# Layer 1's output product with tokens on partitions, and the last norm along the free dimension

## The chip, the cores and the metric

The kernel runs on one core of a Trainium2 chip (trn2). The metric is the device time of one execution in microseconds; runs of the same kernel here lie within 0.1% of each other.

## The reference

Two transformer-like layers over 256 tokens of width 2048, with 256 context tokens beside them. Layer 0 mixes by short convolution and latent attention, layer 1 by grouped attention. What the change touches is the end of layer 1:

```python
y = (attn * silu(p[..., o_v:])) @ w_out                      # 256 x 2048 by 2048 x 2048
z = ALPHA * x + gate * y                                     # gate: one number per channel
mu = jnp.mean(z, axis=-1, keepdims=True)
var = jnp.mean(jnp.square(z - mu), axis=-1, keepdims=True)
x = (z - mu) * lax.rsqrt(var + EPS) * g + b                  # g, b: one number per channel
```

## The kernel before, in words

Channels lie on partitions and tokens along the free dimension from the first load to the store. A product of 2048 channels into 128 is made of 16 steps, one per 128 input channels. Every operand is split into a high and a low fp32r part, and each step is three matmuls (mm3, L128 to L130): high by high, high by low, low by high.

Weights come in transfers of 512 KB into one of three buffers (wraw, in wpieces), issued from SP's queue. A transfer is two pieces of 128 x 512; ACT casts a piece to its high part (L124), DVE subtracts it from the raw numbers for the low part (L125), and four pieces can be ready at a time (WPC). mtile runs the 16 steps of one output tile: here the weights stand still in TensorE and the 256 tokens move, 48 matmuls of 256 columns per tile.

Layer 1 ends with a loop over the 16 tiles of 128 output channels (lines 1130 to 1150). For each tile: the product into PSUM, DVE's residual z = gate * y + z (L1135), ACT's square (L1144), and POOL's running sums of z and of z squared (L1146, L1147). The sums over channels run across partitions, so TensorE makes them with a column of ones (colsum, L197): of tiles 0 to 14 during the last tile's steps, of the last tile behind its product. lnstats and rsqrt (three Newton steps, L180 to L188) work on 128 x 2 numbers on DVE; mean and rstd are broadcast over partitions by transposes (spread, L204), and then DVE, POOL and ACT centre, scale and finish 16 tiles of 128 x 256 (L1157, L1185, L1187, L1189) and SP issues nine stores.

The order of the work: each engine runs its own list of instructions from the front, one after the other, and waits where an operand or a buffer isn't ready. The lists are made at build time from the code's order; in this part of the program a scheduler may move an instruction ahead of others on its engine. PSUM has eight banks, handed out in turn. On DVE's list the splits of coming weights stand between the residuals.

## Time and profile before

| what | us |
|---|---|
| median of 3 runs | 1380.29 (1379.82 to 1380.78) |
| the profiled execution, its own time | 1381.53 |
| its span, first to last instruction | 1379.8 |
| PE busy, share of the span | 1335.0, 97% |
| DVE busy | 1103.2, 80% |
| ACT busy | 600.7, 44% |

The span leaves out what lies before the first and behind the last instruction, so it is shorter than the execution's own time. A busy PE is a PE with a matmul in its pipeline: matmuls overlap, so the time of one is read from start to start, not from its duration. The granted clock (PEclk) is a share of full speed: 1.00 is 2.4 GHz, 0.50 is 1.2 GHz.

### The profile page before, as it was taken

What the parts mean: (1) busy time and instruction counts of PE and PEld (TensorE: products, weight loads), DVE (VectorE), ACT (ScalarE), POOL (GpSimd) and SP (SyncE); (2) the same over time, 40 slices, a digit from 0 to 9 for tenths busy, and PEclk for the clock granted to TensorE, in tenths of its full rate; (3) what the DMA queues carried; (4) which work ended last, traced back from release to release, by engine and by line L of the source; (5) the groups of instructions that cost most, each with busy time, mean ns of one, the idle gap of its engine ahead of it and who ended that gap; (6) DMA issues with size and microseconds to landing.
All of it is one profiled execution on the core that took longest, in us unless ns stands there. A gap on an engine that the chain in (4) does not pass through costs nothing.

```text
span 1379.8 us, 21557 instructions
## 1 busy us (share of the span) xinstructions
PE 1335.0 (97%) x8068; PEld 1165.5 (84%) x8068; DVE 1103.2 (80%) x2037; ACT 600.7 (44%) x1163; POOL 136.1 (10%) x128
## 2 busy tenths in 40 slices
PE   7999999999999999999999999989999999999994
PEld 5667788888878888888888888878999999999994
DVE  7998578576689888888888888889688888887666
ACT  3233356444552222222224333444446666665553
POOL 3354310000000000000000000000330000000333
PEclk9999999999999999999999999999999999999997
DMA  9889412212177665576765688742123434344552
GB/s 366 318 297 340 180 62 77 85 39 84 62 259 247 231 224 215 218 253 214 246 226 177 225 309 329 261 152 81 47 92 124 137 128 144 127 140 137 184 184 77
DMA packets 74473, 251.74 MB, mean 182 GB/s; under 512 B 7616, under 2 KB 10560, under 8 KB 74112
## 3 DMA queue, kind: packets, MB, share of 16 engines
q1 hardware_dynamic: 73168, 243.48, 50.7%
q0 software_dynamic: 1200, 6.88, 1.3%
q8 instruction: 63, 1.03, 0.3%
q14 instruction: 42, 0.34, 0.1%
HBM read 248.24 MB, written 2.10 MB: 181 GB/s over the span
## 4 chain that ended last, share of the span: by engine, by line
PE 84%; DVE 10%; issue 2%; DMA 2%; ACT 1%; SPq 0%; POOL 0%; DVEq 0%; ACTq 0%; POOLq 0%
PE out L130 7%; PE out L128 6%; PE out L129 6%; DVE jk L331 4%; PE g L128 3%; PE g L129 3%; PE g L130 3%; PE q L129 2%; PE q L128 2%; PE q L130 2%; PE cg L130 2%; PE cg L129 2%; PE cg L128 2%; PE cc L129 2%; PE cc L128 2%
## 5 line engine op out<-in xcount | busy, mean ns | idle before, releaser
L124 ACT CAST wh<-wr 128x512 fp32r<-128x512 f32 x468 | 289.9, 621 | 484.1 <-PE out L129 134.2
L125 DVE TENSOR_TENSOR wl<-wr,wh 128x512 fp32r<-128x512 f32 x455 | 316.2, 702 | 140.4 <-ACT wh L124 138.2
L653 DVE CUSTOM_DVE_ANT_0 jk<-gr,sb 128x2048 bf16<-128x2048 f32 x112 | 255.8, 2284 | 4.3 <-DMA gr<-in_wmT_dram 4.1
L128 PE MATMUL out<-mh,wh 128*128 128x512 f32 (+1 forms) x288 | 105.5, 366 | 0.0
L130 PE MATMUL out<-mh,wl 128*128 128x512 f32 (+1 forms) x288 | 105.5, 366 | 0.0
L129 PE MATMUL out<-ml,wh 128*128 128x512 f32 (+1 forms) x288 | 105.2, 365 | 0.0
L129 PE MATMUL g<-xl,wh 128*128 128x256 f32 (+1 forms) x332 | 102.1, 308 | 0.0
L331 DVE CUSTOM_DVE_ANT_0 jk<-wt,srow 128x1024 bf16<-128x1024 f32 x64 | 96.0, 1499 | 5.8 <-DMA wt<-in_wmT_dram 4.1
L1047 POOL TENSOR_TENSOR z<-z,rl 128x256 f32<-128x256 f32 x16 | 13.1, 838 | 792.8 <-ACT rl L1045 792.8
L128 PE MATMUL g<-xl,wh 128*128 128x256 f32 x256 | 75.0, 293 | 0.0
L128 PE MATMUL out<-m1h,wh 128*128 128x256 f32 x256 | 72.5, 283 | 0.0
L129 PE MATMUL out<-m1l,wh 128*128 128x256 f32 x256 | 72.4, 283 | 0.0
L130 PE MATMUL out<-m1h,wl 128*128 128x256 f32 x256 | 72.4, 283 | 0.0
L130 PE MATMUL g<-xl,wl 128*128 128x256 f32 x256 | 72.3, 283 | 0.0
L129 PEld LDWEIGHTS g<-xl,wh 128*128 128x128 f32 x332 | 63.4, 191 | 2.8
L130 PE MATMUL q<-xl,wl 128*128 128x256 f32 x224 | 63.4, 283 | 0.0
L129 PE MATMUL q<-xl,wh 128*128 128x256 f32 x224 | 63.3, 283 | 0.0
L128 PE MATMUL q<-xl,wh 128*128 128x256 f32 x224 | 63.3, 283 | 0.0
L130 PEld LDWEIGHTS out<-mh,wl 128*128 128x128 f32 x288 | 54.3, 188 | 9.0 <-DVE wl L125 0.2
L129 PEld LDWEIGHTS out<-ml,wh 128*128 128x128 f32 x288 | 54.3, 188 | 8.8
L128 PEld LDWEIGHTS out<-mh,wh 128*128 128x128 f32 x288 | 54.3, 188 | 8.6
L130 PE MATMUL cg<-xh,wl 128*128 128x512 f32 x128 | 49.9, 390 | 0.8 <-DVE wl L125 0.8
(332 smaller groups left out, 3658.6 us busy)
## 6 DMA issues: line engine op xcount, KB each, us to landing
gr<-in_wmT_dram SPq DMA_DIRECT2D x64, 1024.0 KB, 5.0
wr<-in_w_o_dram SPq DMA_DIRECT2D x68, 512.0 KB, 3.4
wr<-in_w_g_dram SPq DMA_DIRECT2D x56, 512.0 KB, 3.3
wr<-in_w_c_dram SPq DMA_DIRECT2D x48, 512.0 KB, 4.2
wt<-in_wmT_dram SPq DMA_DIRECT2D x32, 512.0 KB, 6.6
wm<-in_wm_dram SPq DMA_DIRECT2D x32, 512.0 KB, 7.2
wr<-in_w_q_dram SPq DMA_DIRECT2D x32, 512.0 KB, 3.7
xr<-in_xT_dram SPq DMA_DIRECT2D x32, 256.0 KB, 5.8
```

Source lines behind the costliest of these rows:

```text
L124: S.copy(out=pr[0], in_=raw)
L125: (eng or V).tensor_tensor(out=pr[1], in0=raw, in1=f(pr[0]), op=ALU.subtract)
L128: TE.matmul(o, lhsT=a[0], rhs=b[0], start=start, stop=False)
L129: TE.matmul(o, lhsT=a[0], rhs=b[1], start=False, stop=False)
L130: TE.matmul(o, lhsT=a[1], rhs=b[0], start=False, stop=stop)
L331: V.tensor_tensor_reduce(out=junk, in0=rows[hf], in1=srow[v][:, hf * 1024:hf * 1024 + 1024], scale=1.0, scalar=0.0, op0=ALU.mult, op1=ALU.add,
L653: V.tensor_tensor_reduce(out=junk, in0=w, in1=sb[v], scale=1.0, scalar=0.0, op0=ALU.mult, op1=ALU.add, accum_out=dst[:, v:v + 1])
L1047: G.tensor_tensor(out=ax1[j], in0=ax1[j], in1=rl, op=ALU.mult)
```

## The change

The output product is turned round: 128 tokens stand still in TensorE (a column block of mix1) and the weights move. The 16 output tiles become five groups of 4, 4, 4, 2 and 2 tiles (OUT), so a step of a group of four is three matmuls of 512 columns for each of the two token halves. A weight piece is now one input block by four output tiles; each transfer still moves 512 KB, gathered from four places of w_o1 (opieces). The last group's weights are loaded and split during group 2 and kept in buffers of the normed input (xa, xlp) that is no longer read, and its product runs for the first 128 tokens, then for the second.

The output has tokens on partitions, so gate and residual input are turned into that layout by TensorE (turned, 12 transposes in each of the groups 0 to 3). The residual is DVE's multiply with the broadcast gate row and a fused add that also sums z; ACT squares z and sums too (residual). The norm's sums now run along the free dimension on 128 x 2 numbers. normalise(t) makes mean and rstd for one token half, normalises four pieces of 128 x 512, turns each back with four transposes, applies g and b (DVE and ACT, 128 x 128 each) and stores 256 KB per piece. POOL has no part in it. The buffers of keys and values are given back first (kvs.close()), and their room holds the new tiles.

```diff
@@ -36,7 +36,6 @@
 CJ, WSR, WMB, WTB, WQ, XF = 10, 2, 3, 4, 0, 2
 NA = 17
 SK, SR, WS1 = 6, 5, 3
-NPRE, NBET, POOLT, FIN = 3, 1, (3, 4, 6, 8, 11, 12), "AAVAAVAVAVAAAGAV"
 HA, HB, HC = 7, 10, 14
 QH, TH, GS = 4, 5, 3
 
@@ -940,7 +939,8 @@
                             mm3(acc[3 + tt], cols(xc[j], tt * P), cols(w, 0, T), j == 0, j == KT - 1)
             order_.close()
             cgs.close()
-            kvp = ctx.enter_context(right("kv", 18))
+            kvs = ctx.enter_context(ExitStack())
+            kvp = kvs.enter_context(right("kv", 18))
 
 
             dma(gcos, A["gcos"])
@@ -1119,79 +1119,115 @@
                 if h + 1 < NH1:
                     pes = scores1(h + 1, q)
 
-            s1 = s2 = None
-            ln1 = []
-
-            def early1(s1, s2):
-                ln1.append(psum("lst"))
-                colsum(ln1[0], s1, L, 0, "first")
-                colsum(ln1[0], s2, L, 2, "on")
-
-            for m in range(16):
+            kvs.close()
+            oz = ctx.enter_context(right("oz"))
+            grow = oz.tile([P, D], F32, name="grow")
+            zT = [oz.tile([P, D], F32, name=nm("zT")) for _ in range(2)]
+            part = [small.tile([P, 2, 5], F32, name=nm("pt"), tag="part%d" % t) for t in range(2)]
+            OUT = ((0, 4), (4, 4), (8, 4), (12, 2), (14, 2))
+            def opieces(m0, n, make):
+                per = 8 // n
+                for c in range(2):
+                    for i in range(n):
+                        r = wp.tile([P, 1024], F32, tag="wraw", name=nm("wr"), bufs=WRAW)
+                        dma(r.rearrange("p (m k) -> p m k", m=n),
+                            A["w_o1"][m0:m0 + n, c][:, :, i * per * P:(i + 1) * per * P].rearrange("m p k -> p m k"))
+                        rv = r.rearrange("p (m k n) -> p m k n", m=n, k=per)
+                        for u in range(per):
+                            pr = make()
+                            split(rv[:, :, u, :], tuple(x.rearrange("p (m n) -> p m n", m=n) for x in pr))
+                            yield pr
+            def ring_piece():
+                return (wp.tile([P, 512], F32R, tag="wh", name=nm("wh"), bufs=WPC),
+                        wp.tile([P, 512], F32R, tag="wl", name=nm("wl"), bufs=WPC))
+            kept = iter([xa] * 14 + [xlp] * 2)
+            def half_ring():
+                a, b_ = ring_piece()
+                return a[:, :L], b_[:, :L]
+            def kept_piece():
+                t = at(next(kept), F32R, "wo")
+                return t[:, :L], t[:, L:]
+            def turned(m0, n):
+                g_ps = psum("gr")
+                for i in range(n):
+                    TE.transpose(g_ps[:, i * P:i * P + P], gate1[:, m0 + i, :].broadcast_to([P, P]), ident)
+                S.copy(out=grow[:, m0 * P:(m0 + n) * P], in_=g_ps[:, :n * P])
+                for t in range(2):
+                    r_ps = psum("xt")
+                    for i in range(n):
+                        TE.transpose(r_ps[:, i * P:i * P + P], ax1[m0 + i][:, t * P:t * P + P], ident)
+                    S.copy(out=zT[t][:, m0 * P:(m0 + n) * P], in_=r_ps[:, :n * P])
+            def residual(t, i, ps):
+                m0, n = OUT[i]
+                sl = slice(m0 * P, (m0 + n) * P)
+                y = oz.tile([P, T], F32, tag="y", name=nm("y"), bufs=2)[:, :n * P]
+                V.tensor_tensor(out=y, in0=ps[:, :n * P], in1=grow[:, sl], op=ALU.mult)
+                V.tensor_tensor_reduce(out=zT[t][:, sl], in0=y, in1=zT[t][:, sl], scale=1.0, scalar=0.0,
+                                       op0=ALU.add, op1=ALU.add, accum_out=part[t][:, 0, i:i + 1])
+                S.activation(out=y, in_=zT[t][:, sl], func=AF.Square, accum_out=part[t][:, 1, i:i + 1])
+            def normalise(t):
+                e = small.tile([P, 2], F32, name=nm("e"), tag="le2")
+                V.reduce_sum(out=e, in_=part[t], axis=AX.X)
+                V.tensor_scalar(out=e, in0=e, scalar1=1.0 / D, scalar2=None, op0=ALU.mult)
+                q = small.tile([P, 1], F32, name=nm("q"), tag="lq1")
+                V.tensor_mul(q, e[:, 0:1], e[:, 0:1])
+                V.scalar_tensor_tensor(out=q, in0=e[:, 1:2], scalar=EPS, in1=q, op0=ALU.add, op1=ALU.subtract)
+                r = small.tile([P, 1], F32, name=nm("r"), tag="lr1")
+                rsqrt(r, q, 1)
+                mr = small.tile([P, 1], F32, name=nm("mr"), tag="lm1")
+                V.scalar_tensor_tensor(out=mr, in0=e[:, 0:1], scalar=-1.0, in1=r, op0=ALU.mult, op1=ALU.mult)
+                for b_ in range(4):
+                    zn = zT[t][:, b_ * T:b_ * T + T]
+                    V.tensor_scalar(out=zn, in0=zn, scalar1=r, scalar2=mr, op0=ALU.mult, op1=ALU.add)
+                    ps = psum("zt")
+                    for i in range(4):
+                        TE.transpose(ps[:, i * P:i * P + P], zn[:, i * P:i * P + P], ident)
+                    o = oz.tile([P, T], F32, tag="o", name=nm("o"), bufs=4)
+                    for i in range(4):
+                        m, sl = 4 * b_ + i, slice(i * P, i * P + P)
+                        if i % 2:
+                            V.tensor_scalar(out=o[:, sl], in0=ps[:, sl], scalar1=vc("g1", m), scalar2=vc("b1", m),
+                                            op0=ALU.mult, op1=ALU.add)
+                        else:
+                            S.activation(out=o[:, sl], in_=ps[:, sl], func=AF.Identity, bias=vc("b1", m),
+                                         scale=vc("g1", m))
+                    dma(out[4 * b_:4 * b_ + 4, :, t * P:t * P + P].rearrange("m p t -> p m t"),
+                        o.rearrange("p (m t) -> p m t", m=4))
+            late_pieces, last_w = opieces(*OUT[4], kept_piece), []
+            for i in range(4):
+                m0, n = OUT[i]
+                pss = [psum("out1") for _ in range(2)]
+                for k, w in enumerate(opieces(m0, n, ring_piece if n == 4 else half_ring)):
+                    if i == 2:
+                        last_w.append(next(late_pieces))
+                    if k == 8:
+                        turned(m0, 4)
+                    for t in range(2):
+                        mm3(pss[t][:, :n * P], cols(mix1[k], t * P), w, k == 0, k == 15)
+                for t in range(2):
+                    residual(t, i, pss[t])
+            for t in range(2):
                 ps = psum("out1")
-                mtile(ps[:, lat], [A["w_o1"][m, i] for i in range(2)], mix1,
-                      hooks={12: lambda: early1(s1, s2)} if m == 15 else {})
-                zt = ax1[m]
-                V.scalar_tensor_tensor(out=zt, in0=ps[:, lat], scalar=gate1[:, m, :], in1=zt, op0=ALU.mult,
-                                       op1=ALU.add)
-                if m == 0:
-                    ss = tt_(T, F32, "s11")
-                    s1, s2 = ss[:, :L], ss[:, L:]
-                    G.tensor_copy(out=s1, in_=zt)
-                    S.activation(out=s2, in_=zt, func=AF.Square)
-                else:
-                    sq = tt_(L, F32, "sq1")
-                    S.activation(out=sq, in_=zt, func=AF.Square)
-                    if m < 15:
-                        G.tensor_tensor(out=s1, in0=s1, in1=zt, op=ALU.add)
-                        G.tensor_tensor(out=s2, in0=s2, in1=sq, op=ALU.add)
-                    else:
-                        colsum(ln1[0], zt, L, 0, "on")
-                        colsum(ln1[0], sq, L, 2, "last")
-            mean, R = tt_(L, F32, "lb"), tt_(L, F32, "lb")
...
-            _, rr = lnstats(ln1[0], L, early_mean, between)
-            Rp = spread(rr, L)
-            S.copy(out=R, in_=Rp[:, :L])
...
-            for m in range(16):
...
-                    G.tensor_tensor(out=zt, in0=zt, in1=R, op=ALU.mult)
-                    V.tensor_tensor(out=zt, in0=zt, in1=Rp[:, :L], op=ALU.mult)
-                    S.activation(out=o, in_=zt, func=AF.Identity, bias=vc("b1", m), scale=vc("g1", m))
...
+                for k, w in enumerate(last_w):
+                    mm3(ps[:, :2 * P], cols(mix1[k], t * P), w, k == 0, k == 15)
+                residual(t, 4, ps)
+                normalise(t)
 
 
 # ---- launch: the host lays the arrays out ----

```

On PE, at the end of layer 1, before: the last steps of the last tile (out_14075), the column sums (lst), and the two broadcasts of mean and rstd (lbc).

```order
L130 MATMUL out_14075<-m1h_12843,wl_14129 128x256
L128 MATMUL out_14075<-m1h_12976,wh_14128 128x256
L129 MATMUL out_14075<-m1l_12977,wh_14128 128x256
L130 MATMUL out_14075<-m1h_12976,wl_14129 128x256
L197 MATMUL lst_14132<-ones,z_7733 128x1 x4
L204 MATMUL lbc_14157<-ident,lm_14155 128x128 x2
L204 MATMUL lbc_14189<-ident,lr_14172 128x128 x2
```

Now, at the end of the first token half: its last step (out_13853), the 16 transposes of its normalised pieces (zt, from zT_12985), and then the first steps of the second half's product (out_13976).

```order
L127 MATMUL out_13853<-wo_13640,m1h_12976 128x256
L128 MATMUL out_13853<-wo_13640,m1h_12976 128x256
L129 MATMUL out_13853<-wo_13640,m1l_12977 128x256
L1198 MATMUL zt_13929<-ident,zT_12985 128x128 x4
L1198 MATMUL zt_13941<-ident,zT_12985 128x128 x4
L1198 MATMUL zt_13953<-ident,zT_12985 128x128 x4
L1198 MATMUL zt_13965<-ident,zT_12985 128x128 x4
L127 MATMUL out_13976<-wo_13407,m1h_9581 128x256
L128 MATMUL out_13976<-wo_13407,m1h_9581 128x256
```

The transposes of the first half stand ahead of the second half's product in PE's list.

On DVE, at the same place, before: the last low part of the weights, the residual of the last tile (z_7733), the statistics from lst and the start of rsqrt.

```order
L125 TENSOR_TENSOR wl_14129<-wr_14110,wh_14128 128x512
L1135 SCALAR_TENSOR_TENSOR z_7733<-out_14075,gate_76,z_7733 128x256
L243 TENSOR_SCALAR lm_14155<-lst_14132 128x2
L247 TENSOR_SCALAR le_14168<-lst_14132 128x2
L248 TENSOR_TENSOR lq_14167<-lm_14155 128x2
L249 TENSOR_TENSOR lq_14167<-le_14168,lq_14167 128x2
L180 TENSOR_SCALAR rst_14174<-lq_14167 128x2
L182 TENSOR_SCALAR rsy_14173<-rst_14174 128x2
L186 TENSOR_TENSOR rst_14174<-rsy_14173 128x2
```

Now: the first half's residual of the last group (y_13902, then the fused add and sum into zT_12985 and its partial sums pt), the sums (e), the variance (q) and the start of rsqrt.

```order
L1176 TENSOR_TENSOR y_13902<-out_13853,grow 128x256
L1177 ISA zT_12985,pt_12987<-y_13902,zT_12985 128x256
L1177 ISA pt_12987 128x1
L1184 TENSOR_REDUCE e_13906<-pt_12987 128x2
L1185 TENSOR_SCALAR e_13906<-e_13906 128x2
L1187 TENSOR_TENSOR q_13909<-e_13906 128x1
L1188 SCALAR_TENSOR_TENSOR q_13909<-e_13906,q_13909 128x1
L179 TENSOR_SCALAR rst_13914<-q_13909 128x1
L181 TENSOR_SCALAR rsy_13913<-rst_13914 128x1
L185 TENSOR_TENSOR rst_13914<-rsy_13913 128x1
L186 SCALAR_TENSOR_TENSOR rst_13914<-rst_13914,q_13909 128x1
```

The statistics come from pt, which DVE and ACT fill, and no longer from TensorE; the chain of small operations is about as long, and there is one for each token half.

## Rows read from the trace of the kernel before

**Rows 1.** The head of the page.

```profile
span 1379.8 us, 21557 instructions
```

**Rows 2.** Busy time by stretch: length, busy (instructions) per engine, PEclk, DMA share, GB/s.

```profile
1262.00:1357.40 95.40, 95.40 (x798) 95.40 (x797) 56.85 (x83) 46.09 (x81) 26.74 (x29) 1.00 0.47 161
```

**Rows 3.** The view of tile out, layer 1: ns min/median/max, first and last start.

```profile
L128 PE MATMUL out<-m1h,wh x256: 282/283/363, 1265.8 to 1358.4; 128*128 128x256 f32 x128
```

**Rows 4.** The timeline of the end: start, us, engine, line, operation, out<-in.

```profile
1358.67 0.28 PE L130 MATMUL out<-m1h,wl 128*128 128x256 f32 x1
...
1359.06 0.48 DVE L1135 SCALAR_TENSOR_TENSOR z<-out,gate,z 128x256 f32<-128x256 f32 x1 [5.49 <-PE out L130]
...
1366.88 0.16 DVE L187 SCALAR_TENSOR_TENSOR rst<-rst,lq 128x2 f32<-128x2 f32 x1
1367.08 0.16 DVE L188 SCALAR_TENSOR_TENSOR lr<-rst,rsy 128x2 f32<-128x2 f32 x1
...
1376.02 0.41 DVE L1189 TENSOR_SCALAR o<-z,vec 128x256 f32<-128x256 f32 x1
```

**Rows 5.** The timeline of layer 0's output product, PE, 27 steps apart.

```profile
799.66 0.39 PE L130 MATMUL out<-mh,wl 128*128 128x512 f32 x1
...
805.78 0.39 PE L130 MATMUL out<-mh,wl 128*128 128x512 f32 x1
```

**Rows 6.** The chain of waits, layer 1's attention: start, us, what.

```profile
1155.83 0.87 PE pt L1078 x8
```

**Rows 7.** Groups by line and shape, DVE: busy us, mean ns, idle before, releaser.

```profile
L125 DVE TENSOR_TENSOR wl<-wr,wh 128x512 fp32r<-128x512 f32 x455 | 316.2, 702 | 140.4 <-ACT wh L124 138.2
...
L653 DVE CUSTOM_DVE_ANT_0 jk<-gr,sb 128x2048 bf16<-128x2048 f32 x112 | 255.8, 2284 | 4.3 <-DMA gr<-in_wmT_dram 4.1
...
L229 DVE TENSOR_SCALAR pe<-pe,sm 128x512 f32<-128x512 f32 x48 | 23.3, 486 | 1.2
...
L1135 DVE SCALAR_TENSOR_TENSOR z<-out,gate,z 128x256 f32<-128x256 f32 x16 | 7.7, 484 | 9.5 <-PE out L130 9.5
...
L961 DVE TENSOR_TENSOR z<-q,gcos 128x256 f32<-128x256 f32 x14 | 5.8, 417 | 0.0
...
L1013 DVE TENSOR_SCALAR kr<-k,vec 128x256 f32<-128x256 f32 x4 | 1.9, 473 | 0.0
```

**Rows 8.** Groups by line and shape, ACT.

```profile
L124 ACT CAST wh<-wr 128x512 fp32r<-128x512 f32 x468 | 289.9, 621 | 484.1 <-PE out L129 134.2
...
L1144 ACT ACTIVATE z<-z 128x256 f32<-128x256 f32 x15 | 6.3, 418 | 7.8 <-DVE z L1135 6.7
...
L224 ACT ACTIVATION_READ_ACCUMULATOR pe<-sc,bs,qrs 128x1 f32 x32 | 6.1, 191 | 0.0
...
L327 ACT COPY part<-pm 128x128 f32<-128x128 f32 x16 | 4.3, 266 | 44.9 <-PE pm L324 44.9
```

**Rows 9.** Busy time by stretch, where the granted clock stays or changes.

```profile
915.00:918.00 3.00, 0.70 (x5) 0.21 (x3) 2.67 (x13) 1.11 (x3) 0.00 (x0) 1.00 0.00 0
...
926.00:927.00 1.00, 0.48 (x2) 0.34 (x2) 0.96 (x4) 0.51 (x1) 0.00 (x0) 0.82 0.59 117
...
930.00:931.00 1.00, 1.00 (x6) 0.82 (x5) 1.00 (x3) 0.51 (x1) 0.00 (x0) 0.97 0.66 255
...
1363.00:1364.00 1.00, 0.00 (x0) 0.00 (x0) 1.00 (x3) 0.00 (x0) 1.00 (x2) 0.78 0.03 8
```

**Rows 10.** The timeline of PE at half clock, 256 columns.

```profile
927.68 0.41 PE L921 MATMUL acc<-xl,wsh 128*128 128x256 f32 x1
927.89 0.41 PE L922 MATMUL acc<-xl,wsl 128*128 128x256 f32 x1
```

**Rows 11.** The view of tile wr in 1262 to 1357: weight transfers.

```profile
DMA to landing us min/median/max: 3.0/3.3/4.4
```

**Rows 12.** Busy time by stretch: weights in 4 KB runs, the output in 1 KB runs.

```profile
820.00:880.00 60.00, 60.00 (x266) 49.67 (x266) 50.72 (x62) 20.54 (x38) 0.00 (x0) 1.00 0.84 313
...
1377.00:1378.00 1.00, 0.00 (x0) 0.00 (x0) 0.00 (x0) 0.00 (x0) 0.00 (x0) 0.50 1.00 341
```

More of the change, by code (lines that the diff above doesn't have):

```diff
@@ L1151, in mixer_kernel @@
-            mean, R = tt_(L, F32, "lb"), tt_(L, F32, "lb")
-            pool_tiles = set(POOLT)
-            fast = [m for m in range(16) if m not in pool_tiles]
-            def centre(m):
-                e = G if m in pool_tiles else V
-                e.tensor_tensor(out=ax1[m], in0=ax1[m], in1=mean, op=ALU.add)
-            def early_mean(m):
-                mp = spread(m, L)
-                S.copy(out=mean, in_=mp[:, :L])
-                for i in sorted(pool_tiles):
-                    centre(i)
@@ L1165, in mixer_kernel @@
-            ahead = iter(fast)
-            def between():
-                for _ in range(NBET):
-                    centre(next(ahead))
-            _, rr = lnstats(ln1[0], L, early_mean, between)
-            Rp = spread(rr, L)
-            S.copy(out=R, in_=Rp[:, :L])
-            late = set(ahead)
-            for m in range(16):
-                if m in late:
-                    with tc.issue_after(last_rs[0]):
-                        centre(m)
-                if m % 2 == 0:
-                    o2 = tt_(T, F32, "o")
-                zt, o = ax1[m], o2[:, (m % 2) * L:(m % 2) * L + L]
-                if m in pool_tiles:
-                    G.tensor_tensor(out=zt, in0=zt, in1=R, op=ALU.mult)
-                else:
-                    V.tensor_tensor(out=zt, in0=zt, in1=Rp[:, :L], op=ALU.mult)
-                if FIN[m] == "A":
-                    S.activation(out=o, in_=zt, func=AF.Identity, bias=vc("b1", m), scale=vc("g1", m))
-                else:
-                    (V if FIN[m] == "V" else G).tensor_scalar(
-                        out=o, in0=zt, scalar1=vc("g1", m), scalar2=vc("b1", m), op0=ALU.mult, op1=ALU.add)
-                if m < 2:
-                    dma(out[m], o)
-                elif m % 2:
-                    dma(out[m - 1:m + 1].rearrange("m p t -> p m t"), o2.rearrange("p (m t) -> p m t", m=2))
```

## Prediction

> **What bounds the kernel now.** I read the head of the page, then the busy time of one stretch, then the last 25 us as a timeline, then prices by group, then the clock.
>
> The profiled execution has a span of 1379.8 us [rows 1]. Layer 1's output product is TensorE's alone: from 1262 to 1357.4 PE is busy 95.40 us of 95.40 at clock 1.00, while DVE has 57 and ACT 46 [rows 2]. Its first matmul starts at 1265.8 [rows 3], its last at 1358.67 [rows 4]: 768 matmuls of 256 columns in 93.0 us, 0.120 us each with 0.8 us of column sums between them. I call the end of the last one's slot, 1358.8, the product's end. Behind it lie 21.0 us in which PE does next to nothing: residual, statistics, mean and rstd broadcast, 16 tiles finished. The last tile ends at 1376.43 and the span 3.4 us later [rows 4].
>
> So two things count: when the product ends, and how long the chain behind it is.
>
> **The change part by part.** (All against the span of 1379.8. The profiled execution's own time is 1381.5, the median of the runs 1380.3; I add the sum's difference to the median.)
>
> *The products.* The weights now move, 512 columns at once. Layer 0's output product shows that shape at 27 steps in 6.12 us, 0.2267 us each [rows 5], against 2 x 0.120 here. Groups 0 to 2: 288 x 0.2267 = 65.3 us. Group 3 has 256 columns: 96 x 0.120 = 11.5. Group 4 for the first token half: 48 x 0.120 = 5.8. Sum 82.6.
>
> *Transposes added under the products.* turned() puts 12 on PE per group, 48 in all. Eight cost the chain 0.87 us [rows 6], so 48 x 0.109 = 5.2 us, not hidden, since PE is the bound.
>
> *Splits.* As many columns as before: 0.62 us on ACT and 0.70 on DVE per 512 [rows 7, 8], per 1.36 us of PE. In group 2 the kept pieces come on top (256 columns, DVE 0.42 as the row of that width says [rows 7]): 1.12 of 1.36 us, still hidden. At the start of group 3 DVE has y, y, reduce, reduce of 512 columns in its queue ahead of the fourth piece; the last y waits for group 2's end, then 0.27 + 0.7 + 2 x 0.75 + 0.42 = 2.9 us, while PE has 3 pieces x 0.72 us and two matmuls of the fourth = 2.4. A stall of 0.5 us. POOL's 26 us of sums [rows 2] go; nobody waited for them but the end.
>
> *Weight transfers.* 512 KB as before, but in runs of 1 KB instead of 4. Group 2 wants 12 of them in 16 x 1.36 = 21.8 us, 289 GB/s. Runs of 4 KB gave 313 GB/s at a share of 0.84; the output's runs of 1 KB gave 341 at 1.00 [rows 12]. That is enough, at 0.85 of the engines. I cost it at nothing; bounds 0 and 3 us (a rival).
>
> First half's product end: 1265.8 + 82.6 + 5.2 + 0.5 = **1354.1**.
>
> *First half finished.* Here the order on PE decides: the 16 transposes of the first half stand ahead of the second half's 48 products, so PE waits for the norm. The chain: from product end to DVE 0.27 [rows 4]; y of 256 columns 0.42 [rows 7]; the fused add and sum, not seen at this size, between 0.3 (256 of 2048 columns at 2284 ns) and 0.48 (a scalar_tensor_tensor of 256): 0.5 with its accumulator read; ACT's square 0.42 and its accumulator read 0.19 [rows 8], with handovers 0.1. That is 1.9 us. Then 16 small DVE operations (reduce, scale, two for the variance, 11 of rsqrt, one for mean times rstd) at 0.195 from start to start [rows 4] = 3.1; the first normalised piece 0.49 [rows 7]; handover 0.06. **5.6 us** in which PE stands still, where before the second half followed at once.
>
> *The transposes themselves.* At full clock they hide behind the four pieces (0.49 each, against 4 x 0.109): PE goes on 7.5 us after the product end. At half clock they don't: a matmul of 256 columns then steps by 0.21 instead of 0.12 [rows 10], so 4 transposes cost 0.78 and PE goes on after 5.6 + 3.1 = 8.7 us.
>
> *Which clock.* After 1358.8 PE did only sums and a broadcast, and the granted clock fell from 2.4 to 1.2 GHz in 1363 to 1364, 5 us later; at 926.6 it fell, with PE busy 0.48 of that microsecond, and it came back at 930.1, 3.4 us later, with PE busy throughout. Against that, in 915 to 918 PE was busy 0.70 of 3.00 us and the clock stayed at 1.00 [rows 9]. A gap of 5.6 us is nearer to the first. The Trainium skill (page "TensorE: Matmul & The Clock Gate", section "Why this matters for your kernels") tells authors to leave no idle gap between bursts of matmuls, because one gap puts the clock back to half; by that rule the sum below stands, by the row of 915 to 918 it is 3.2 us less. I take the low clock, with 3.4 us of it falling on the second half's products: 16 steps at 0.213, 16 x 0.093 = 1.5 us more. Bounds 0 and 48 x 0.093 = 4.5.
>
> *Second half's products* 48 x 0.120 + 1.5 = 7.3 us.
>
> *Second half's end*, with nothing to hide it: the same 5.6, then at half clock 3.1 for the transposes, 0.3 to DVE and ACT, and the last of their eight 128x128 operations each. DVE's form is not seen at this size: between half of 0.473 (256 columns from PSUM) and 0.473 [rows 7]; ACT's copy of it takes 0.27 [rows 8]; I take 0.3 and 3 of them behind the last transpose, 0.9. Then 3.4 to the end of the span [rows 4]. Sum 13.3, against 21.0 now; at full clock DVE's queue sets it (5.1 + 4 x 0.49 + 8 x 0.3 + 3.4 = 12.8).
>
> Sum: 1354.1 + 8.7 + 7.3 + 13.3 = **1383.4**, 3.6 us over the span before. With the median: 1380.3 + 3.6 = **1383.9 us**.
>
> In short: the tail shrinks by 7.7 and the products by 3.8 (with the sums 4.6), but transposes cost 5.2, a stall 0.5, the wait in the middle 8.7 and the clock 1.5.
>
> **The rivals.**
> 1. *The clock holds.* For it: 915 to 918 [rows 9]; against it: the two falls. 1354.1 + 7.5 + 5.8 + 12.8 = 1380.2, with the median 1380.7: no change that can be told.
> 2. *The weights starve PE.* A buffer's round is landing 3.3 us, two casts 1.24, the last subtraction 0.7, issue 0.3 = 5.5; three buffers give one per 1.85 us, and group 2 wants one per 1.81. If every transfer lands in 4.4, the slowest now [rows 11], it is one per 2.2: 12 x 0.4 = 4.8 us, less some 2 us of pieces split ahead, about 3 us on top: 1387.
> 3. *Faster: the chain from product end to first normalised piece is short.* It is paid twice, so it decides: at 5.6 us each and full clock the change is even; at 4.0 or less with the clock held (two operations' starts 0.13 apart instead of 0.195, the accumulators read in passing) it gives 2 x 1.6 us back: 1377.5. Against it: the 0.195 stands in the trace.
> 4. *The half is finished under the products as meant*, without PE's wait. The instruction order excludes it: PE runs its list in order, and the transposes come first. Only the 128x128 operations and the stores of the first half run under products.
>
> **How the numbers follow.** A measurement of this kernel tells about 0.2% from no change, 2.8 us: faster is below 1377.5, slower above 1383.1. The forecast (clock falls) has 0.55; with its bounds it spans 1381 to 1387, and about 0.42 of it lies above 1383.1. Rival 1 has 0.2, nearly all within 0.2%. Rival 2 has 0.15, slower. Rival 3 has 0.1, of which 0.08 is below 1377.5. So slower 0.57, same 0.35, faster 0.08. The range leaves out rival 3 and the far ends: 1379.5 to 1387.5.
>
> **What would show it.** In the new profile: PE's products at 0.227 us apart to about 1354; an idle PE of 5 to 6 us there, ended by DVE's zT; the second half's products starting 7.5 to 9 us after the first half's end; a granted clock of 0.5 in them; the last out_dram issue some 10 us behind the last product. I am wrong if products of the second half run while DVE is in the first half's rsqrt, if PE waits for wh or wl for more than 2 us in group 2, or if the chain to the first zT is under 4 us.

## The result and the profile after

The changed kernel took 1388.66 us (median of 4 runs, 1388.22 to 1390.56), the kernel before beside it 1380.53 (1379.82 to 1381.72): a ratio of 1.0061, 95% interval 1.0043 to 1.0078. It is slower, as forecast, but by 8.1 us where 3.6 were forecast, and 1388.66 lies 1.2 us above the range. The profiled execution took 1388.77 us, its span is 1386.6.

Where the new product stage begins and when its kept weights (the last group's) are first used, in the view of tile out of the changed kernel (ns min/median/max, first and last start, shapes):

```profile
L127 PE MATMUL out<-wh,m1h x128: 277/389/501, 1264.4 to 1349.7; 128*128 128x512 f32 x96, 128*128 128x256 f32 x32
...
L127 PE MATMUL out<-wo,m1h x32: 283/283/562, 1350.0 to 1371.3; 128*128 128x256 f32 x32
```

It starts at 1264.4, 1.4 us sooner than in the profiled execution before [rows 3], though nothing ahead of it was changed: the profiled runs of this document, whose programs are the same up to there, start it between 1263.4 and 1265.9. Groups 0 to 3 take 85.6 us; the prediction's own terms for them give 65.3 + 11.5 + 5.2 + 0.5 = 82.5. The busy time by stretch (length, busy and instructions per engine, PEclk, DMA share, GB/s) shows where the other 3.1 us lie:

```profile
1262.00:1290.00 28.00, 28.00 (x142) 23.73 (x141) 15.47 (x26) 13.94 (x25) 0.00 (x0) 1.00 0.53 169
1290.00:1310.00 20.00, 20.00 (x96) 16.73 (x95) 11.41 (x21) 11.59 (x24) 0.00 (x0) 1.00 0.59 183
1310.00:1335.00 25.00, 23.54 (x104) 17.77 (x103) 16.00 (x33) 14.66 (x33) 0.00 (x0) 1.00 0.70 219
...
1357.00:1362.00 5.00, 0.72 (x4) 0.72 (x5) 3.87 (x19) 0.51 (x2) 0.00 (x0) 0.85 0.00 0
1362.00:1368.00 6.00, 6.00 (x32) 6.00 (x31) 3.69 (x10) 3.33 (x8) 0.00 (x0) 0.55 0.43 118
```

Before, PE was busy through the whole stage [rows 2]. Now it has gaps in 1310 to 1335, which is group 2, the group that also loads and splits the kept weights. By the starts of its matmuls, groups 0 and 1 take 23.1 us each and group 2 takes 26.4 (1310.6 to 1337.0); since matmuls overlap, less of that shows as idle time. The timeline of PE at the first gap:

```profile
1318.47 0.39 PE L128 MATMUL out<-wl,m1h 128*128 128x512 f32 x1
1318.70 0.39 PE L129 MATMUL out<-wh,m1l 128*128 128x512 f32 x1
1319.49 0.50 PE L127 MATMUL out<-wh,m1h 128*128 128x512 f32 x1 [0.41 <-ACT wh L123]
1320.22 0.50 PE L128 MATMUL out<-wl,m1h 128*128 128x512 f32 x1 [0.23 <-DVE wl L124]
1320.56 0.39 PE L129 MATMUL out<-wh,m1l 128*128 128x512 f32 x1
```

Two steps of 0.227 became 0.79 and 0.73: PE waits for a piece that ACT has only just cast and DVE only just subtracted. ACT itself waited for the transfer, and the transfer had waited for its buffer, as the rows of the three engines ahead of the gap show:

```profile
1311.72 1.15 ACT L123 CAST wh<-wr 128x512 fp32r<-128x512 f32 x2 [2.15 <-DMA wr<-in_w_o_dram]
1312.38 0.69 DVE L124 TENSOR_TENSOR wl<-wr,wh 128x512 fp32r<-128x512 f32 x1 [1.45 <-ACT wh L123]
1312.99 0.68 DVE L1177 CUSTOM_DVE_ANT_0 zT<-y,zT 128x512 f32<-128x512 f32 x1
...
1314.20 0.68 DVE L124 TENSOR_TENSOR wl<-wr,wh 128x512 fp32r<-128x512 f32 x1
...
1314.91 0.37 SPq L94 DMA_DIRECT2D wr<-in_w_o_dram  x1
...
1318.82 1.14 ACT L123 CAST wh<-wr 128x512 fp32r<-128x512 f32 x2 [1.35 <-DMA wr<-in_w_o_dram]
```

The transfer is issued at 1314.91, when the second subtraction out of a buffer ends (1314.88). Between the two subtractions DVE's list has two operations of group 1's residual, so the buffer came free some 1.2 us later than its casts allowed. In the view of waits (1262 to 1387: us in total, times, longest):

```profile
PE zt L1198 <- DVE zT L1195: 10.6, 2, 5.3
ACT wh L123 <- DMA wr<-in_w_o_dram: 6.3, 5, 2.2
...
PEld out L128 <- DVE wl L124: 2.4, 6, 0.5
DVE o L1203 <- ACT o L1206: 2.0, 6, 0.4
PEld out L127 <- ACT wh L123: 1.9, 3, 0.8
```

Its first row is the chain, paid twice as predicted. PE's timeline in the middle and at the end:

```profile
1355.66 0.28 PE L129 MATMUL out<-wo,m1l 128*128 128x256 f32 x1
1361.28 3.68 PE L1198 MATMUL zt<-ident,zT 128*128 128x128 f32 x16 [5.34 <-DVE zT L1195]
1364.61 0.56 PE L127 MATMUL out<-wo,m1h 128*128 128x256 f32 x1
...
1371.54 0.28 PE L129 MATMUL out<-wo,m1l 128*128 128x256 f32 x1
1377.09 3.68 PE L1198 MATMUL zt<-ident,zT 128*128 128x128 f32 x16 [5.27 <-DVE zT L1195]
```

A slot of a product is 0.12 us, so the first half's product ends at 1355.78 and the second's at 1371.66. Step by step against the prediction:

| step | predicted, us | measured, us |
|---|---|---|
| first product's start | 1265.8 | 1264.4 |
| to the first half's product end | 88.3 | 91.4 |
| to the second half's first product | 8.7 | 8.8 |
| second half's products | 7.3 | 7.05 |
| second half's end, to the end of the span | 13.3 | 14.9 |
| end of the span | 1383.4 | 1386.6 |

The differences are -1.4, +3.1, +0.1, -0.25 and +1.65, in sum 3.2 us, while the median lies 4.8 above the forecast. The other 1.6 belong to no step: the execution profiled before was 1.2 us above its median and the one profiled after 0.1, and 2.2 us of an execution now lie outside its span where 1.7 did. The -1.4 is most likely no gain of the change either, but the late start of the execution profiled before. So the wait in the middle and the half clock came as forecast; what was missed is the starved group 2 and the end. The clock, by stretch:

```profile
1359.00:1360.00 1.00, 0.00 (x0) 0.00 (x0) 0.83 (x6) 0.00 (x0) 0.00 (x0) 1.00 0.00 0
1360.00:1361.00 1.00, 0.00 (x0) 0.00 (x0) 0.86 (x5) 0.00 (x0) 0.00 (x0) 0.77 0.00 0
...
1364.00:1367.00 3.00, 3.00 (x16) 3.00 (x15) 2.46 (x7) 2.16 (x6) 0.00 (x0) 0.50 0.52 141
1367.00:1368.00 1.00, 1.00 (x9) 1.00 (x9) 0.00 (x0) 0.00 (x0) 0.00 (x0) 0.82 1.04 287
```

It goes to half within 1360 to 1361, after some 5 us with nothing on PE, and comes back in 1367 to 1368, 6 us after the transposes and 3 us after the products set in. That is the rule of the Trainium skill that the prediction weighed (page "TensorE: Matmul & The Clock Gate", section "Why this matters for your kernels": no idle gap between bursts), and this trace agrees with it.

### The profile page after: what moved, and what is told of

The parts are those of the page before. It is cut to its first block, busy times and chain, and to the rows that moved or that the text cites. A ratio compares the mean times of both kernels' runs of the same rounds, so it can differ in the third digit from the quotient of the medians.

```text
span 1386.6 us, 21064 instructions
## 1 busy us (share of the span) xinstructions
PE 1344.6 (97%) x7840; PEld 1161.3 (84%) x7840; DVE 1101.1 (79%) x2083; ACT 606.9 (44%) x1199; POOL 99.4 (7%) x86
## 5 line engine op out<-in xcount | busy, mean ns | idle before, releaser
L123 ACT CAST wh<-wr 128x512 fp32r<-128x512 f32 (+1 forms) x468 | 285.5, 614 | 474.7 <-PE out L128 92.3
L124 DVE TENSOR_TENSOR wl<-wr,wh 128x512 fp32r<-128x512 f32 (+1 forms) x455 | 306.8, 683 | 143.6 <-ACT wh L123 141.1
L129 PE MATMUL cu<-xh,wl 128*128 128x512 f32 x128 | 49.9, 390 | 0.3 <-DVE wl L124 0.3
L129 PE MATMUL cb<-xh,wl 128*128 128x512 f32 x128 | 49.9, 390 | 0.3 <-DVE wl L124 0.3
L127 PE MATMUL cb<-xh,wh 128*128 128x512 f32 x128 | 49.8, 389 | 0.0
```

The costliest lines, as they stand in the source:

```text
L123: S.copy(out=pr[0], in_=raw)
L124: (eng or V).tensor_tensor(out=pr[1], in0=raw, in1=f(pr[0]), op=ALU.subtract)
L127: TE.matmul(o, lhsT=a[0], rhs=b[0], start=start, stop=False)
L129: TE.matmul(o, lhsT=a[1], rhs=b[0], start=False, stop=stop)
```

## The experiments

Times are medians; each ratio is against runs of the kernel before on the same chip, whose median there was between 1380.5 and 1381.0. The runs of one kernel spread further than the 0.1% named at the start: those of the kernel before by up to 0.23% (1379.91 to 1383.07). "Groups 0 to 3" is the time from the first product to the first use of the kept weights (82.5 by the prediction's terms), "end" that from the last product's start to the end of the span. Both are from the profiled run.

| kernel | us | ratio, 95% interval | groups 0 to 3 | end |
|---|---|---|---|---|
| changed | 1388.66 | 1.0061 (1.0043 to 1.0078) | 85.6 | 15.1 |
| e1 order | 1380.64 | 0.9997 (0.9988 to 1.0006) | 87.5 | 15.9 |
| e5 no halves | 1384.62 | 1.0028 (1.0018 to 1.0038) | 85.6 | 21.4 |
| e4 PE kept busy | 1387.35 | 1.0045 (1.0030 to 1.0060) | 87.6 | 14.8 |
| e3 pieces spread | 1384.70 | 1.0023 (1.0011 to 1.0035) | 82.5 | 15.1 |
| e2 long runs | 1387.48 | 1.0046 (1.0029 to 1.0062) | 86.4 | 15.1 |
| e7 no kept loads | 1386.64 | 1.0045 (1.0030 to 1.0060) | 82.3 | 18.0 |
| e8 four buffers | 1386.21 | 1.0036 (1.0024 to 1.0049) | 84.0 | 15.0 |
| e6 banks | 1387.41 | 1.0050 (1.0036 to 1.0063) | 85.2 | 14.5 |
| e9 order and spread | 1376.39 | 0.9964 (0.9951 to 0.9976) | 82.9 | 15.9 |
| b3 three changes | 1377.82 | 0.9975 (0.9967 to 0.9984) | 84.7 | 14.9 |
| b4 and PE kept busy | 1376.63 | 0.9972 (0.9962 to 0.9982) | 85.8 | 15.1 |
| b5 best | 1373.94 | 0.9949 (0.9935 to 0.9962) | 82.3 | 14.5 |

**e1, the order on PE.** normalise(t) is cut in two: statistics and normalised rows stay, transposes, o and stores become finish(t).

```diff
                 residual(t, 4, ps)
+                if t:
+                    finish(0)
                 normalise(t)
+            finish(1)
```

(In finish, `if i % 2` becomes `if i % 2 and t`, so the first half's o are all ScalarE's.)

> The first half's transposes, o operations and stores are put behind the second half's products; only its statistics and normalisation stay ahead of them. Theory of the order (the change does not do what it is for, because TensorE stands through the first half's chain): the second half's products start right behind the first half's, without the 5.5 us of idle time and the 3.7 us of half-clock transposes, and run at full clock, 5.8 us instead of 7.05; the last product ends about 1361.5 to 1362 us instead of 1371.66. The last wait of 5.4 us then holds the first half's 16 transposes and o operations. Time about 1379 to 1380.5 us, 8 to 9.5 us less than the changed kernel. Rival, the wait only moves (the second half's chain queues behind the first half's o operations on ScalarE): last product about 1361.5 us, but the second half's first transposed piece 8 us or more behind it instead of 5.4, time 1383 to 1385 us. Rival, the middle wait is not on the path: time as the changed kernel, 1388.7 us.

Measured 1380.64 us, 8.0 less and just above the 1379 to 1380.5 expected. PE's timeline around the second half:

```profile
1363.12 0.28 PE L129 MATMUL out<-wo,m1l 128*128 128x256 f32 x1
1363.24 1.91 PE L1203 MATMUL zt<-ident,zT 128*128 128x128 f32 x16
1369.46 3.68 PE L1203 MATMUL zt<-ident,zT 128*128 128x128 f32 x16 [4.31 <-DVE zT L1195]
```

PE never stops between the halves: the second half's 48 products take 5.8 us, and the first half's 16 transposes take 1.91 at full clock in place of 3.68. The middle lost 8.8 us and the products 1.2; 0.8 came back in a longer end, and 1.9 in this run's longer stall of groups 0 to 3: 7.3 net, and 7.6 is what the spans differ by. The last product is thus at 1363.1 and not at the 1361.5 expected. The longer end has a place in DVE's timeline:

```profile
1362.39 1.92 DVE L1195 TENSOR_SCALAR zT<-zT,r,mr 128x512 f32<-128x512 f32 x4
1364.22 0.42 DVE L1176 TENSOR_TENSOR y<-out,grow 128x256 f32<-128x256 f32 x1
```

The first half's four normalised pieces run on DVE until 1364.2 and hold up the second half's residual by 0.8 us, since its last matmul had ended at 1363.4. So the theory of the order holds, and both rivals fall.

**e5, no halves at the end.** Both halves' last products side by side, then both ends.

```diff
+            pss = [psum("out1") for _ in range(2)]
+            for k, w in enumerate(last_w):
+                for t in range(2):
+                    mm3(pss[t][:, :2 * P], cols(mix1[k], t * P), w, k == 0, k == 15)
...
+            for t in range(2):
+                normalise(t)
+            for t in range(2):
+                finish(t)
```

> The last group is not halved: both token halves' products of the last two output blocks run side by side as in the other groups, and both halves are normalised, transposed and stored behind them. Theory that halving pays only if the order is right (in the changed kernel the first half's end delays the second half's products by 8.8 us): the last product ends about 1361.5 us, the end behind it holds both halves' statistics, transposes and o operations and is some 6 to 8 us longer than the 14.9 us of the changed kernel; time 1382 to 1385 us, so 4 to 6 us less than the changed kernel though nothing is finished under products, and 2 to 4 us more than the kernel with the halved but reordered end (1380.6). Rival, halving pays as it stands: 1389 us or more.

1384.62 us, as expected: the end grows by 6.3 us, the middle wait goes, and it is 4.0 us better than the halves as the change orders them. Halving pays only in e1's order, by 4.0 us.

**e4, PE kept busy through the waits.**

```diff
                 residual(t, 4, ps)
+                dm = psum("dm")
+                for k in range(38):
+                    TE.matmul(dm[:, :2 * P], lhsT=mix1[k % 16][0][:, t * P:t * P + P], rhs=last_w[k % 16][0],
+                              start=True, stop=True)
                 normalise(t)
```

> 38 further 256-column products into a spare bank, whose result nobody reads, are put on TensorE behind each half's last product, to keep it at work for some 4.5 us of the 5.5 us wait for the normalised rows. Nothing else is changed. Theory of the clock (the wait costs its own 5.5 us and besides the half clock behind it): the granted clock stays 1.00 through both waits, the transposes of each half take 1.9 us instead of 3.7 (partly hidden behind the pieces of the normalisation), the second half's products 5.8 instead of 7.05; in all about 3 to 4 us less, 1385 us. Rival, the transposes are paced by the normalised pieces and not by the clock: only the products' 1.25 us come back, 1387.5 us. Rival, the further products hold up the transposes: 1389 us or more.

```profile
1358.15 0.28 PE L129 MATMUL out<-wo,m1l 128*128 128x256 f32 x1
1358.27 4.72 PE L1232 MATMUL dm<-wo,m1h 128*128 128x256 f32 x38
1363.79 2.09 PE L1198 MATMUL zt<-ident,zT 128*128 128x128 f32 x16 [0.79 <-DVE zT L1195]
1365.63 0.36 PE L127 MATMUL out<-wo,m1h 128*128 128x256 f32 x1
```

The clock stays at 1.00 from 1357 to 1380. The second half starts 7.4 us behind the first half's end in place of 8.8 (the prediction's 7.5 at full clock), and its products take 5.8 in place of 7.05: 2.7 us is what the half clock cost in the middle. The end gained only 0.3, and the run's stall was 2.0 us longer than the changed kernel's, so the time shows 1.3 us, inside the intervals. The mechanism is shown; the 3 to 4 us are not.

**e3, the kept pieces spread.**

```diff
-                    if i == 2:
+                    if i < 3 and (16 * i + k) % 3 == 0:
                         last_w.append(next(late_pieces))
```

> The last two groups' weight pieces, which are all split during the third group's products (one kept piece beside each ring piece, so that ScalarE, VectorE and the transfers have double work there), are split one for every three steps of the first three groups instead. Theory of the peak demand (third group starved since two splits and half more bytes fall on each step): the 3.0 us of gaps in 1310 to 1335 us go to under 0.7, the waits of ScalarE for the weight transfers (6.3 us) with them, the last product of the first half starts about 1352.7 instead of 1355.66 and the time is 2.5 to 3.2 us less, about 1386. Rival, demand is even but the transfers lag by their latency at every piece: the gaps spread out over three groups and the time stays within 0.7 us of 1388.7.

(The kept pieces are those of the last group alone, and group 2 has half more bytes to load and columns to split with them, not double.) The stall is gone: groups 0 to 3 take 82.5 us, the figure that the prediction's terms give, and by stretch:

```profile
1310.00:1335.00 25.00, 25.00 (x117) 20.53 (x116) 14.70 (x28) 13.37 (x29) 0.00 (x0) 1.00 0.66 207
```

4.0 us less, more than expected: the second half's products also got the full clock back sooner in this run (6.2 us in place of 7.05).

**e2, long runs.** The host lays the weights out so that a transfer reads 4 KB at a time.

```diff
-                        dma(r.rearrange("p (m k) -> p m k", m=n),
...
+                        dma(r, A["w_o1"][2 * m0 + c * n + i])
```

> The output weights are laid out on the host so that each 512 KB transfer reads 4 KB in one run instead of 1 KB or 512 B runs; the products, their order and every other instruction stay. Theory of the run length (the transfers land late because of their short runs: 3.8 us against 3.3 before): transfers land in 3.3 us or less, the idle time of TensorE in 1310 to 1335 us goes from 3.0 to under 1 us, and the time falls by 2 to 3 us to about 1386. Theory of the buffers (three staging buffers are not enough for the demand of the third group, whatever the run length): the landing may shorten by some tenths, the gaps stay near 3 us, the time stays within 0.7 us of 1388.7. Theory of the queue's own rate (219 GB/s is what the transfers get at this demand): as the theory of the buffers.

86.4 us for groups 0 to 3, so the stall stays, though the transfers land a little sooner (median 4.1 us in 1310 to 1335, against 4.4). The 1.2 us in the time lie inside the intervals. The theory of the run length falls.

**e7, without the kept loads.** The transfers of the kept pieces go, their splits stay in group 2, pinned behind the ring's splits.

```diff
-                        dma(r.rearrange("p (m k) -> p m k", m=n),
+                        own or dma(r.rearrange("p (m k) -> p m k", m=n),
```

> The four transfers of the last two output blocks' weights into the staging buffers are left out, and their 16 pieces are split from a tile that is loaded once, one piece behind each ring piece of the third group as before; so two output blocks of 16 are computed from the wrong weights. ScalarE, VectorE and TensorE have the same work in the third group, the transfers a third less (256 KB instead of 384 KB a step). Theory that transfers and staging buffers starve the third group: the gaps of TensorE in it (1.5 to 3 us so far, some 3.1 us up to the first half's last product) go to under 0.5 us, the time falls by 2.5 to 3.5 us to about 1385.5. Theory that the splits starve it: gaps and time stay, 1388 to 1389 us.

```profile
1310.00:1335.00 25.00, 25.00 (x124) 21.10 (x123) 19.33 (x42) 16.71 (x39) 0.00 (x0) 1.00 0.56 170
```

ACT and DVE are busier than in the changed kernel and PE has no gap: the work of the splits is not the cause, the transfers and their buffers are. (The edit also fixes the order of the splits, one kept piece behind each ring piece, where the changed kernel has up to four kept ones in a row; what that alone does is not shown.) Its time gives back only 2.0 us, since the tile took the room of two o buffers and the end grew to 18.0; in its view of waits from 1355 on:

```profile
ACT o L1220 <- DMA out_dram<-o: 5.5, 4, 2.4
```

**e8, a fourth buffer.**

```diff
-                        r = wp.tile([P, 1024], F32, tag="wraw", name=nm("wr"), bufs=WRAW)
+                        turn.append(0)
+                        r = (oz.tile([P, 1024], F32, tag="wk", name=nm("wk"), bufs=1) if len(turn) % 4 == 0 else
+                             wp.tile([P, 1024], F32, tag="wraw", name=nm("wr"), bufs=WRAW))
```

> Every fourth weight transfer of the output product goes into a fourth staging buffer, so that four buffers go round instead of three; the bytes, the third group's double demand and the shape of the transfers stay (the scheduler draws some kept splits forward by a few pieces). To make room the first half has two o buffers instead of four, and the second half's o lie in the gate's rows. Theory that the round of three buffers starves the third group (the transfers' queue stood 57.6 us waiting for a buffer's last subtraction, and the DMA share falls to 0.05 in single microseconds ahead of the gaps): the gaps up to the first half's last product fall from 3.1 to under 1 us. Theory that the rate of the transfers is the limit (219 GB/s in the third group): the gaps stay at 2.5 us or more, and the transfers land later than 4.4 us. Time by the first 1385.5 to 1386.5 us, by the second 1388 to 1389.

Groups 0 to 3 take 84.0: half of the stall is left. The time lies in the range of the first theory, but the gaps are at neither theory's number. For the buffers speak single microseconds of the changed kernel: the transfers nearly stop ahead of the stall at 1318.7, while from 1313 to 1314 they moved 395 GB/s, more than the 289 that group 2 wants:

```profile
1313.00:1314.00 1.00, 1.00 (x7) 0.81 (x6) 1.00 (x4) 0.29 (x1) 0.00 (x0) 1.00 1.05 395
1314.00:1315.00 1.00, 1.00 (x6) 0.62 (x4) 1.00 (x3) 1.00 (x4) 0.00 (x0) 1.00 0.57 217
1315.00:1316.00 1.00, 1.00 (x6) 0.83 (x6) 1.00 (x3) 0.94 (x2) 0.00 (x0) 1.00 0.05 12
```

But e8 also drew some kept splits forward, so the shares of buffers and transfer rate stay open.

**e6, whole banks.** `if i % 2` becomes `if b_ % 2`.

> Only who does the o operations changes: each PSUM bank's four pieces are done by one engine (ScalarE the even banks, VectorE the odd ones), where ScalarE and VectorE took turns piece by piece within a bank. Theory of the shared bank (the two engines wait for each other piece by piece, so that the o operations of a half end 0.5 to 1 us late): the last o operation comes 0.5 to 1 us sooner behind the last product than the 10.6 us of the changed kernel, and the time falls by that, to about 1388 us; each piece takes 0.33 to 0.37 us instead of 0.41 to 0.46. Rival, the pieces are paced by the half-clock transposes and the taking of turns costs nothing: no difference.

Groups by line in the second half's end (busy us, mean ns), first the changed kernel, then e6:

```profile
L1206 ACT ACTIVATE o<-zt,vec 128x128 f32<-128x128 f32 x8 | 3.3, 454 | 5.6 <-issue 4.9 <-PE zt L1198 0.4
L1203 DVE TENSOR_SCALAR o<-zt,vec 128x128 f32<-128x128 f32 x8 | 3.1, 409 | 1.2 <-ACT o L1206 1.0
```

```profile
L1206 ACT ACTIVATE o<-zt,vec 128x128 f32<-128x128 f32 x8 | 3.0, 456 | 5.1 <-issue 4.9 <-ACT o L1206 0.2
L1203 DVE TENSOR_SCALAR o<-zt,vec 128x128 f32<-128x128 f32 x8 | 2.7, 403 | 1.0 <-PE zt L1198 1.0
```

DVE no longer waits for ACT, and eight operations take 3.0 and 2.7 us where they took 3.3 and 3.1. The time of one is the same (456 and 403 ns), not the 0.33 to 0.37 us expected; they only overlap more on their own engine. The end is 0.6 us shorter, as expected; the time's 1.2 us lie inside the intervals.

**e9, order and spread.** The edits of e1 and e3.

> The two changes that each gave back time alone, and nothing else: the first half's transposes, o operations and stores behind the second half's products (8.0 us less alone), and the kept pieces split one every three steps (4.0 us less alone). If the wait of TensorE and the starved third group are separate causes, the savings add: 1388.7 - 8.0 - 4.0 = 1376.7 us. If one hides the other: 1379 to 1380.6 us.

1376.39 us against 1376.7: the savings add, so the two causes are separate, and the kernel is faster than the one before, by 0.36% (0.24 to 0.49).

**b3, b4, b5, what the end still gives.** b3 takes e1's order with another spread of the pieces, shares the first half's normalised pieces between DVE and ACT, and does the second half's o by whole banks:

```diff
+                    if t == 0 and b_ % 2:
+                        S.activation(out=zn, in_=zn, func=AF.Identity, bias=mr, scale=r)
...
+                    if 16 * i + k in range(8, 48) and (16 * i + k) % 5 in (0, 2):
```

> Three changes of the order together: the first half's transposes, o operations and stores behind the second half's products (1380.6 us alone), the kept pieces split over three groups instead of one (4 us less alone), and in the end the first half's normalisation shared between VectorE and ScalarE, ahead of the second half's residual, which it held up by 0.86 us, and o operations of the second half by whole banks on one engine each. Theory that the two causes add (one is the wait of TensorE through the first half's chain, the other the starved third group): 8 + 4 us less than the changed kernel and about 1 us from the end, 1375 to 1377 us, 4 to 5 us less than the kernel before. Rival, the two share one cause or the spread pieces cost elsewhere: 1379 us or more.

The end is 1.0 us shorter than e9's, but the denser spread brought a stall back (84.7), so it is no better than e9: 1377.82 us, between the 1375 to 1377 of the theory and the 1379 of the rival. b4 adds 28 of e4's products between the two halves' transposes:

> The kernel of the three changes together, with 28 further 256-column products on TensorE between the first half's transposes and the second half's, so that it works through most of the last wait. Theory of the clock: the second half's 16 transposes run at full clock, paced by the four pieces of the normalisation (about 2.2 us instead of 3.7), 1 to 1.5 us less than without them, 1374 to 1375.5 us. Rival, the end is bound by the o operations of the two engines (ScalarE has 16 of the first half to finish by then) and not by the transposes: 0 to 0.5 us less.

The clock holds and the second half's transposes take 2.09 us, yet the end isn't shorter: ACT waits 1.4 us for a store to give back an o buffer. The 1.2 us in the time lie inside the intervals, so the theory's 1 to 1.5 us are not shown. b5 takes e3's spread, lets the o operations alternate by bank and writes them over the gate's rows, so no store is waited for:

```diff
-                    o = oz.tile([P, T], F32, tag="o", name=nm("o"), bufs=4)
+                    o = grow[:, b_ * T:b_ * T + T] if t else oz.tile([P, T], F32, tag="o", name=nm("o"), bufs=4)
```

> From the kernel with the further products in the last wait (1376.6 us): the kept pieces one every three steps from the first group on, where no gap was left, instead of two every five from the ninth step on, where 1.5 to 2.3 us of gaps were left; the second half's o operations alternate between the engines bank by bank and write into the gate's rows, which are no longer needed, so that none waits for a store. Theory: 1.5 to 2 us from the gaps, 0.5 to 1 us from the end, 1374 to 1375 us. Rival, the end is bound by the eight stores one behind the other and the gaps come back elsewhere: 1376 us or more.

```profile
1357.58 0.28 PE L129 MATMUL out<-wo,m1l 128*128 128x256 f32 x1
1357.70 1.91 PE L1209 MATMUL zt<-ident,zT 128*128 128x128 f32 x16
1359.36 3.60 PE L1247 MATMUL dm<-wo,m1h 128*128 128x256 f32 x28
1363.08 2.09 PE L1209 MATMUL zt<-ident,zT 128*128 128x128 f32 x16
```

1373.94 us, 0.51% (0.38 to 0.65) below the kernel before and 14.7 us below the changed one. Groups 0 to 3 are at 82.3, the end at 14.5.

## Why the prediction was wrong in size

**Right: the wait in the middle.** The order on PE was read as the fact that decides, the chain was priced at 5.6 us and measured at 5.5 (1355.78 to 1361.28), and PE went on after 8.8 where 8.7 stood. e1 shows that this order alone, with the clock behind it, costs 8.0 us. Rivals 3 and 4 are out: the 16 small DVE operations do step by 0.195 (1357.57 to 1360.68), and no product of the second half ran in the wait.

**Right: the clock.** Rival 1 (the clock holds) is out; "16 x 0.093 = 1.5 us more" measured 1.2 (7.05 against e4's 5.8). That the size came so close is in part luck: the clock fell in every profiled run with this wait, but in the others (e7, e3, e2, e8, e6) the second half's products took 5.8 to 6.7 us, since it came back sooner. In e7, whose transposes begin at 1357.72 and products at 1360.77:

```profile
1360.00:1361.00 1.00, 1.00 (x9) 1.00 (x8) 0.76 (x2) 0.87 (x3) 0.00 (x0) 0.76 0.00 0
```

**Right: the products and their transposes.** Without the stall, groups 0 to 3 take 82.3 to 82.5 us (e3, e7, b5) against 82.5.

**Wrong: "Weight transfers ... That is enough, at 0.85 of the engines. I cost it at nothing".** The rate was compared with the best rates seen, 313 and 341 GB/s, which other stages had with another demand. Group 2 got 219 with three buffers going round, and lost 3.1 us. Rival 2 had the mechanism and the size (3 us, 1387) but a chance of 0.15; what it needed, a transfer of 4.4 us every time, was near the usual case in group 2, where the transfers' median landing was 4.4 (3.3 is the median of the whole stage before [rows 11]):

```profile
wr<-in_w_o_dram SPq DMA_DIRECT2D x12, 512.0 KB, 4.4
```

The term's comparison of 1 KB with 4 KB runs had nothing to do with it (e2). Rival 2's round also has a buffer emptied in 1.24 + 0.7 = 1.9 us; the one shown above took 3.2 (1311.72 to 1314.88), with the residual in between. The prediction counted that queue of DVE at the start of group 3 and not at the start of group 2. No run takes the residual out, so its part is read off the timeline and not shown by an experiment. The prediction's sign of being wrong, PE waiting more than 2 us for wh or wl in group 2, came true: PE's weight loads (PEld) waited 2.4 and 1.9 us, nearly all of it there.

**Wrong: "Second half's end ... Sum 13.3".** The chain in it is 5.43 (1371.66 to 1377.09) against 5.6. Behind the first transpose stood 3.1 + 0.3 + 0.9 = 4.3 us to the last o operation; it was 5.6 (DVE's last, below, ends at 1382.69):

```profile
1382.28 0.41 DVE L1203 TENSOR_SCALAR o<-zt,vec 128x128 f32<-128x128 f32 x1 [0.18 <-ACT o L1206]
```

An o operation takes 0.41 on DVE and 0.45 on ACT, not 0.3, and the two engines take turns within a bank, which costs the 0.6 us that e6 gives back. The last stores then took 3.9 us and not 3.4.

**The range.** Its upper end, 1387.5, took in rival 2 or the bounds of the clock, but not the starved group together with a longer end, each of which the text had bounds for.

## What to carry to other kernels

Work that is to hide under products must stand behind them in the list of the engine that runs the products; a half that is finished ahead of the other half's products stops the engine for its whole chain. When a change raises a stage's demand for weights (here by half), price the round of the staging buffers at that demand, with the other work that stands between the splits, not the best rate of another stage, and spread the loading over the stages that have room. A cost that looks hidden on each engine should be checked once more with the transfers that feed it.

## What the runs showed of the hardware that was not expected

- ACT and DVE did not read one PSUM bank side by side: in the changed kernel DVE's o operations waited six times for ACT's (2.0 us in all), in e6's view of waits there is none. The profile infers such waits from semaphore events, so it is the program that holds the engines apart here. In e6 each engine has not only a bank but also the o buffer to itself, so which of the two the program guards is not shown. The Trainium skill (page "PSUM — Partial Sum Buffer", section "PSUM bank collisions raise a hardware error") says that the hardware doesn't stall there and that programs are to guard a bank by semaphores, which no run here tests.
- Stores in 512 B runs moved less at the same share of the DMA engines than the 1 KB runs before (341 GB/s at 1.00 [rows 12]):

```profile
1384.00:1385.00 1.00, 0.00 (x0) 0.00 (x0) 0.00 (x0) 0.00 (x0) 0.00 (x0) 0.71 1.06 283
```

- The stall of group 2 differs from run to run of the same stage: groups 0 to 3 took 85.2 to 87.6 us in the five profiled runs that left this stage as the change has it (changed, e1, e4, e5, e6).
